# Two load slots and three store regions, and a TensorE program with a loop, in a transpose of 8192 x 8192 float32

## The chip, the cores and the metric

The kernel runs on one core of one Trainium2 chip. A core has TensorE (PE in the profile, its weight loads PEld), VectorE (DVE), ScalarE (ACT), GpSimd (POOL) and SyncE (SP), which here does nothing but issue transfers, and 16 DMA engines that move data between HBM and SBUF. The metric is the device time of one execution in microseconds (us); lower is better.

## The reference

```python
def setup_inputs():
    return {
        "x": np.random.randn(8192, 8192).astype(np.float32),
    }

def reference(x: np.ndarray) -> np.ndarray:
    return np.transpose(x)
```

256 MB are read and 256 MB written, and every element changes its place; no arithmetic is done.

## The kernel before

**Chunks and pieces.** The input is cut into T = 128 chunks. Chunk t is a block of 128 rows (block c = t % 64) by 4096 columns (half s = t // 64), 16 KB in each of 128 partitions, 2 MB; `load(t)` (L81) brings it in with one DMA. A chunk has NR = 16 pieces, one for each range r of 256 columns (J = 4096 columns, PIECE = 256 floats in a partition). TensorE transposes a piece in two matmuls against the identity (L113): one takes the even columns, one the odd, so that partition q of the result holds output rows 2q and 2q + 1, 128 columns of each. A chunk is thus 32 transposes, 16 into the PSUM tensor ps0 and 16 into ps1.

**Stores.** One piece would make output rows of just 512 bytes. So pieces of the same range r wait in the buffer `slots` (120 pieces) until 16 chunks have given theirs; `store(w)`, with r = w % 16, then writes 16 pieces as output rows of 8 KB, 2 MB in all. The ranges are staggered: with every chunk t exactly one range becomes complete, that of store t. The first 15 stores are short (1 to 15 pieces), and a flush of 15 short stores comes after the last chunk. Chunk 64 begins the second half of the columns, and the stores around it are written in two DMAs.

**What runs for chunk t.** TensorE takes the ranges in the order (t + g) % 16 for g = 0 to 15 (L112), so that the first piece, g = 0, is the one that completes store t. `gather(t)` (L196) makes VectorE copy the 15 older pieces of store t out of `slots` into a place in `arena` (L216); it first waits until the earlier store in that place has left (L203). `copies(t)` (L225) moves the new pieces out of PSUM: ScalarE those of ps0 (g = 0 to 7), VectorE those of ps1 (g = 8 to 15) (L247). Piece g = 0 goes straight into the store's place, by ScalarE; the others go to `slots`, into room that the gather has just emptied, so ScalarE first waits for the gather (semaphore s_g, L228). TensorE signals (s_pe) after 2, 4, 8, 12 and 16 pieces (`GO`), and begins each half of the next chunk when the copies have emptied that half of PSUM (L108).

**The arena.** It has NIN = 3 load slots of 16 pieces and FIN = 38 pieces for stores, a little over two full stores. A planner at build time (L152 to L167) gives every store a place in these 38 pieces, taking the one that comes free first, and lists in `before` whose end the gather must wait for. The stores of the last two chunks and of the flush may also take load slots.

**Order on SP.** SP issues every DMA, in program order on one queue, and waits in that order too (L281 to L294): store t (after the direct piece's copy, s_cl, L255), then the next load, which waits until TensorE has finished the chunk that was in its slot (L289). Up to chunk 15 and near the end this is load t + 3, whose slot chunk t has just left; between them load t + 2, whose slot chunk t - 1 left. TensorE's program is written out in full: 4096 transposes.

Of the kernel before, what the change touches and what calls it, by code (L numbers as in the profile page):

```python
# [40 lines left out]
def kernel(  # L41
# [15 lines left out]
    NIN = 3  # L57
# [3 lines left out]
    FIN = 38  # L61
    GO = (2, 4, 8, 12, 16)
    assert CH % W == 0

    with tc.tile_critical():  # L65
# [3 lines left out]
        arena = nc.alloc_sbuf_tensor("arena", [P, NIN * J + FIN * PIECE], dt).ap()  # L69
        ins = [arena[:, k * J:(k + 1) * J] for k in range(NIN)]  # L70
# [3 lines left out]
        s_ld = [nc.alloc_semaphore(f"s_ld{k}") for k in range(NIN)]  # L74
        s_st = [nc.alloc_semaphore(f"s_st{k}") for k in range(2 * W - 1)]
        s_pe = nc.alloc_semaphore("s_pe")
        s_cp = [nc.alloc_semaphore("s_cpa"), nc.alloc_semaphore("s_cpv")]
        s_g = nc.alloc_semaphore("s_g")
        s_cl = nc.alloc_semaphore("s_cl")

        def load(t):  # L81
            s, c = divmod(t, CH)
            nc.sync.dma_start(
                out=ins[t % NIN], in_=x[c * P:(c + 1) * P, s * J:(s + 1) * J]
            ).then_inc(s_ld[t % NIN], 16)

        for t in range(NIN):
            load(t)

        nc.gpsimd.memset(ident, 0.0).then_inc(s_id, 1)  # L90
        nc.gpsimd.wait_ge(s_id, 1)
        nc.gpsimd.affine_select(  # L92
            out=ident,
            in_=ident,
            compare_op=mybir.AluOpType.not_equal,
            fill=1.0,
            base=0,
            pattern=[[-1, P]],
            channel_multiplier=1,
        ).then_inc(s_id, 1)  # L100


        nc.tensor.wait_ge(s_id, 2)
        for t in range(T):
            for g in range(NR):
                h, u = divmod(g, NR // 2)
                if u == 0 and t:
                    nc.tensor.wait_ge(s_cp[h], t)  # L108
                if g == 0:
                    nc.tensor.wait_ge(s_ld[t % NIN], 16 * (t // NIN + 1))  # L110
                q = (t + g) % NR
                for b in range(B):  # L112
                    tr = nc.tensor.transpose(  # L113
                        pss[h][:, (u * B + b) * P:(u * B + b + 1) * P],
                        ins[t % NIN][:, q * PIECE + b:(q + 1) * PIECE - B + b + 1:B],
                        ident,
                    )
                if g + 1 in GO:
                    tr.then_inc(s_pe, 1)


        def lane(w):
            return w % W if w < T else W + w - T

        def parts(w):
            first, last = max(0, w - W + 1), min(w, T - 1)
            cut = [first] + [t for t in range(first + 1, last + 1) if t % CH == 0] + [last + 1]
            return list(zip(cut[:-1], cut[1:]))

        def cells(w):  # L130
            return sum(z - a for a, z in parts(w))
# [9 lines left out]

        flush = []
        for k in range((W - 1) // 2):
            flush += [T + W - 2 - k, T + k]
        flush.append(T + (W - 1) // 2)
        order = list(range(T)) + flush

        users = []
        home = {}
        before = {}  # L150
        end = NIN * NR + FIN
        for n, w in enumerate(order):  # L152
            size = cells(w)
            best = None
            low = NIN * NR if w < T - 2 else 0
            for o in range(low, end - size + 1):
                over = [(u, when) for u, a, z, when in users if a < o + size and o < z]
                for k in range(NIN):
# [133 lines left out]
        for w in flush:  # L292
            gather(w, T)
            store(w)  # L294
# [32 lines left out]
```

## Time and profile before

| | |
|---|---|
| median of 3 runs | 1276.58 us (1276.57 to 1276.77) |
| the profiled execution: its own time | 1278.0 us |
| its span, first to last instruction | 1276.2 us |
| moved by DMA | 537.53 MB, 421 GB/s over the span |
| loads | 128 of 2,048 KB, 17.2 us from issue to landing (median) |
| full stores | 98 of 2,048 KB, 13.0 us (median) |
| TensorE, VectorE, ScalarE busy | 57%, 47%, 22% of the span |
| mean granted TensorE clock | 0.741 of full speed |

Times within the profile count from the start of the span. The page gives the busy share of each engine, the span in 40 slices with the rate in GB/s, the DMA queues (q1 is SP's data queue; the queues of kind "instruction" bring the engines' code), the chain of waits that ended last, and groups of instructions by line. The trace behind it answers for stretches of the span: busy times and rate by stretch, waits by who waited for whom, instructions in order of time, and the time from issue to landing of the DMAs of one line.

### The profile page before, as it was taken

The numbers are of one execution on the slowest core, as the hardware profiler recorded it, in microseconds if no ns is written. First come the engines' busy times: TensorE is split into PE (matmuls) and PEld (weight loads), VectorE is DVE, ScalarE is ACT, GpSimd is POOL, SyncE is SP. The second block draws the span as 40 slices with busy tenths as digits, with TensorE's granted clock in tenths as the row PEclk, the third lists the DMA queues.
The fourth block names the chain that finished last, engine by engine and source line by source line (L and its number), as shares of the span: only waits on it lengthen the run. The fifth ranks groups of instructions, "written<-read, shape, count | busy, mean of one in ns | idle before, by whom it ended". The sixth has DMA issues, their size and how long they took to land.

```text
span 1276.2 us, 10252 instructions
## 1 busy us (share of the span) xinstructions
PE 731.6 (57%) x4096; PEld 711.1 (56%) x4096; DVE 600.5 (47%) x662; ACT 285.5 (22%) x513; POOL 0.7 (0%) x6
## 2 busy tenths in 40 slices
PE   5674456655665566556665665556656655555630
PEld 5664455655665556556665665556655655555630
DVE  3542644445445444454455444544454444454471
ACT  3321222222222222222222222222222222222210
POOL 0000000000000000000000000000000000000000
PEclk9987777677777777777678677686776787677765
DMA  9999999999999999999999999999999999999999
GB/s 388 428 426 388 384 429 430 430 430 430 431 430 429 427 428 429 427 420 430 415 425 421 427 427 424 422 429 430 428 426 426 425 426 423 426 425 426 424 386 375
DMA packets 41358, 537.53 MB, mean 421 GB/s; under 512 B 4576, under 2 KB 5216, under 8 KB 8288
## 3 DMA queue, kind: packets, MB, share of 16 engines
q1 hardware_dynamic: 41312, 536.89, 99.7%
q8 instruction: 32, 0.52, 0.1%
q14 instruction: 14, 0.11, 0.0%
HBM read 268.44 MB, written 268.44 MB: 421 GB/s over the span
## 4 chain that ended last, share of the span: by engine, by line
DMA 82%; PE 7%; issue 2%; DVE 2%; SPq 2%; ACT 1%; ACTq 0%; DVEq 0%
DMA arena<-in_x_dram 77%; PE ps L113 7%; DMA out_dram<-arena 5%; SPq L28 2%; ACT arena L247 1%; DVE arena L216 1%; DVE slots L247 1%; ACTq L233 0%; DVEq L212 0%; DVEq L210 0%; SPq L322 0%; DVEq L233 0%; SPq L65 0%
## 5 line engine op out<-in xcount | busy, mean ns | idle before, releaser
L113 PE MATMUL ps<-ident,arena 128*128 128x128 f32 x4096 | 731.6, 360 | 499.7 <-DMA arena<-in_x_dram 472.5
L113 PEld LDWEIGHTS ps<-ident,arena 128*128 128x128 f32 x4096 | 711.1, 218 | 519.8 <-issue 485.8
L247 DVE COPY slots<-ps 128x1024 f32<-128x1024 f32 (+3 forms) x344 | 307.6, 946 | 604.5 <-PE ps L113 604.2
L216 DVE COPY arena<-slots 128x2048 f32<-128x2048 f32 (+7 forms) x318 | 303.3, 1004 | 48.6 <-DMA out_dram<-arena 27.1
L247 ACT COPY slots<-ps 128x256 f32<-128x256 f32 (+2 forms) x384 | 249.8, 661 | 134.4 <-PE ps L113 126.7
L247 ACT COPY arena<-ps 128x256 f32<-128x256 f32 x128 | 47.6, 372 | 809.9 <-PE ps L113 722.5
L247 ACT ACT_TABLE_LOAD x1 | 1.3, 1283 | 0.9 <-SPq L65 0.9
L92 POOL TENSOR_SCALAR_AFFINE_SELECT ident<-ident 128x128 f32<-128x128 f32 x1 | 0.3, 292 | 0.2 <-POOL ident L90 0.2
L90 POOL MEMSET ident<- 128x128 f32 x1 | 0.2, 204 | 0.5 <-SPq L65 0.5
L311 POOL MEMSET const-bfloat16-1.0<- 128x1 bf16 x1 | 0.1, 101 | 0.0
L311 POOL MEMSET const-uint8-127<- 128x1 uint8 x1 | 0.1, 101 | 0.0
L311 POOL MEMSET const-float32-0.0<- 128x1 f32 x1 | 0.1, 98 | 0.2 <-issue 0.2
L311 POOL MEMSET const-float32-1.0<- 128x1 f32 x1 | 0.1, 98 | 0.0
## 6 DMA issues: line engine op xcount, KB each, us to landing
arena<-in_x_dram SPq DMA_DIRECT2D x128, 2048.0 KB, 17.2
out_dram<-arena SPq DMA_DIRECT2D x98, 2048.0 KB, 13.0
out_dram<-arena SPq DMA_DIRECT2D x4, 1920.0 KB, 11.3
out_dram<-arena SPq DMA_DIRECT2D x4, 1792.0 KB, 11.6
out_dram<-arena SPq DMA_DIRECT2D x4, 1664.0 KB, 12.7
out_dram<-arena SPq DMA_DIRECT2D x4, 1536.0 KB, 12.7
out_dram<-arena SPq DMA_DIRECT2D x4, 1408.0 KB, 13.7
out_dram<-arena SPq DMA_DIRECT2D x4, 1280.0 KB, 13.7
```

What stands on the lines that cost most here:

```text
L28: return eng.add_instruction(mybir.InstDMACopy(mode="Copy", name=nc.get_next_instruction_name(), engine=eng.engine, ins=[physical(in_)], o ...
L90: nc.gpsimd.memset(ident, 0.0).then_inc(s_id, 1)
L92: nc.gpsimd.affine_select(out=ident, in_=ident, compare_op=mybir.AluOpType.not_equal, fill=1.0, base=0, pattern=[[-1, P]], channel_multipl ...
L113: tr = nc.tensor.transpose(pss[h][:, (u * B + b) * P:(u * B + b + 1) * P], ins[t % NIN][:, q * PIECE + b:(q + 1) * PIECE - B + b + 1:B], i ...
L216: cp = nc.vector.tensor_copy(out=ap(arena, do, [[P, len(v)], [dist, B], [1, P]]), in_=ap(slots, so, [[gap, len(v)], [P, B], [1, P]]),)
L247: cp = eng.copy(out=dst, in_=i) if e == 0 else eng.tensor_copy(out=dst, in_=i)
L311: nc = _bacc.Bacc("TRN2", target_bir_lowering=False, num_devices=1)
```

## The change

1. The arena has 86 pieces as before, but another plan: two load slots of 16 pieces and 54 pieces for stores, a little over three full stores. Two more places of 16 pieces, in the store area, serve as load slots for the first chunks: up to chunk 4 loads run four ahead, up to chunk 9 three ahead, then two ahead. The store area is 22 pieces up to store 5, 38 up to store 10, and 54 from there. Stores before the flush lie in the store area; those of the flush may also take load slots.
2. SP's order: load t + 2 follows store t - 1 (before: store t). It waits until TensorE has finished chunk t, which was in its slot.
3. The planner sorts loads and stores by when they want room, and a list `before` for each names the earlier users of that room, loads and stores alike.
4. TensorE takes the ranges of a chunk in fixed order 0 to 15 (the last chunk alone is rotated as before), and signals after 4, 8, 12 and 16 pieces. So the direct piece of store t is ScalarE's when t % 16 < 8 and VectorE's otherwise, and store t waits for all of that engine's copies of chunk t (s_cpa or s_cpv). A gather waits for the copies of both engines.
5. TensorE's semaphores are counted down by TensorE itself (s_ld, and new ones, s_free, that ScalarE and VectorE raise after waiting for their own copies), so that its instructions are alike in every round. Chunks 0 to 11 are written out, a loop whose body is two chunks runs 57 times (chunks 12 to 125), and the last two chunks are written out.
6. The flush has another order: store 128 first, whose last piece also goes straight from PSUM, then 142, 129, 141, 130 and so on.

The core of the diff:

```diff
-    NIN = 3
-    FIN = 38
-    GO = (2, 4, 8, 12, 16)
+    FIN = 54
+    E = 12
+    FOUR, THREE = 5, 10
+    END = 2 * NR + FIN
+
+    def lead(t):
+        return 4 if t < FOUR else 3 if t < THREE else 2
...
+    slot_of = {ends[0][1]: 54, ends[1][1]: 70, ends[2][1]: 0, ends[3][1]: NR}
...
+    for t in range(T):
+        if t:
+            order.append(("S", t - 1))
+        while loaded <= min(T - 1, t + lead(t)):
+            order.append(("L", loaded))
+            loaded += 1
+    order += [("S", T - 1)] + [("S", w) for w in flush]
...
+    for _, k, size, until in sorted(wanted):
+        if k[0] == "L":
+            o = spot(k[1])
+        else:
+            w = k[1]
+            lo = 2 * NR if w < T - 1 else 0
+            hi = 54 if w < over[0] else 70 if w < over[1] else END
+            late = lambda o: max([f for _, a, z, f in users if a < o + size and o < z], default=0)
+            o = min(range(lo, hi - size + 1), key=lambda o: (late(o), o))
+        home[k] = o
+        before[k] = sorted({u for u, a, z, _ in users if a < o + size and o < z}, key=lambda u: due[u])
...
         def load(t):
             s, c = divmod(t, CH)
+            o = home["L", t] * PIECE
+            for u in before["L", t]:
+                free(nc.sync, u)
...
             if runs:
-                nc.vector.wait_ge(s_cp[0], upto)
-                if w >= T:
-                    nc.vector.wait_ge(s_cp[1], upto)
+                for k in range(2):
+                    nc.vector.wait_ge(s_cp[k], upto)
...
                 cp.then_inc(s_cp[e], 1)
+                if t < T - 1:
+                    eng.wait_ge(s_cp[e], t + 1)
+                    eng.sem_inc(s_free[e], 1)
 
         def store(w):
-            if w < T:
-                nc.sync.wait_ge(s_cl, w + 1)
+            if w == T - 1:
+                nc.sync.wait_ge(s_x, 1)
+            elif w < T:
+                nc.sync.wait_ge(s_cp[w % NR // (NR // 2)], w + 1)
             else:
+                if w == T:
+                    nc.sync.wait_ge(s_cp[0], T)
                 nc.sync.wait_ge(s_g, ready[w])
...
+        def transposes(t):
+            o = home["L", t]
+            for g in range(NR):
+                h, u = divmod(g, NR // 2)
+                if u == 0:
+                    nc.tensor.sem_inc(s_free[h], -1).wait_op(s_free[h], 1, "sem-ge")
+                if g == 0:
+                    nc.tensor.sem_inc(s_ld[o], -16).wait_op(s_ld[o], 16, "sem-ge")
+                q = (o + range_at(t, g)) * PIECE
...
+        nc.tensor.wait_ge(s_id, 2)
+        for t in range(E):
+            transposes(t)
...
+        with nc.body("turns", valid_engines=pe):
+            for t in range(E, E + 2):
+                transposes(t)
+            nc.regs_alu(turn, turn, 1, op=mybir.AluOpType.add)
+            nc.tensor.br_lt(turn, (T - 2 - E) // 2, on_true="turns", on_false="done")
+        nc.switch_bb("done")
+        for t in range(T - 2, T):
+            transposes(t)
```

259 lines of the change are left out of this document (144 added, 115 removed).

## The prediction

> **What bounds the kernel now.** I read the page first: the busy shares, the slices of the span and the DMA queues.
>
> ```profile
> span 1276.2 us, 10252 instructions
> PE 731.6 (57%) x4096; PEld 711.1 (56%) x4096; DVE 600.5 (47%) x662; ACT 285.5 (22%) x513; POOL 0.7 (0%) x6
> GB/s 388 428 426 388 384 429 430 430 430 430 431 430 429 427 428 429 427 420 430 415 425 421 427 427 424 422 429 430 428 426 426 425 426 423 426 425 426 424 386 375
> q1 hardware_dynamic: 41312, 536.89, 99.7%
> q8 instruction: 32, 0.52, 0.1%
> q14 instruction: 14, 0.11, 0.0%
> ```
>
> No compute engine is busy over 57% of the span, and the data queue q1 fills 99.7% of the 16 DMA engines. The 536.89 MB are input plus output, and the change moves the same bytes. So the time is bytes over rate, and a gain can only come out of slices below the best rate, which is 430 GB/s or a little over. Where they lie, I read from busy times in stretches that I cut at those slices (last column GB/s, before it the DMA share and the TensorE clock):
>
> ```profile
> core 0: us, PE busy (x) PEld busy (x) DVE busy (x) ACT busy (x) POOL busy (x), PEclk, DMA share, GB/s
> 0.00:10.00 10.00, 1.60 (x8) 1.63 (x9) 0.00 (x0) 1.74 (x3) 0.70 (x6) 1.00 0.78 315
> 10.00:100.00 90.00, 63.22 (x442) 61.08 (x440) 43.65 (x53) 27.10 (x51) 0.00 (x0) 0.91 1.01 426
> 100.00:160.00 60.00, 25.63 (x160) 25.09 (x160) 30.13 (x34) 12.52 (x24) 0.00 (x0) 0.70 0.96 383
> 160.00:400.00 240.00, 145.00 (x779) 141.16 (x780) 112.51 (x122) 54.95 (x99) 0.00 (x0) 0.73 1.01 430
> 400.00:1210.00 810.00, 481.13 (x2627) 467.88 (x2626) 384.05 (x419) 183.73 (x329) 0.00 (x0) 0.74 1.01 425
> 1210.00:1230.00 20.00, 13.73 (x81) 13.38 (x80) 10.79 (x11) 4.76 (x10) 0.00 (x0) 0.76 0.89 368
> 1230.00:1270.00 40.00, 1.30 (x7) 0.90 (x5) 19.40 (x24) 0.73 (x1) 0.00 (x0) 0.50 1.01 418
> 1270.00:1276.20 6.20, 0.00 (x0) 0.00 (x0) 0.00 (x0) 0.00 (x0) 0.00 (x0) 0.50 0.47 197
> ```
>
> Against 430 the stretches lose, length times (1 - rate/430): start 2.7 us, 10 to 100 0.8, 100 to 160 **6.6**, 160 to 400 nothing, 400 to 1210 **9.4**, 1210 to 1230 **2.9**, then 1.1 and 3.4. That is 26.9 us in all. The start (nothing to move yet), the stores alone and the last landing stay as they are, 7.2 us. The three bold ones, 18.9 us, are what this change can touch.
>
> How deep the queue is, the chain of waits shows, at its beginning and at one chunk of the good stretch, and the landings of stores there (from 160 to 400 us):
>
> ```profile
> 0.96 7.30 DMA arena<-in_x_dram
> ...
> 250.23 0.14 issue
> 250.36 1.11 PE ps L113 x4
> ...
> 251.95 0.54 SPq L28
> ...
> 252.54 17.20 DMA arena<-in_x_dram
> ```
> ```profile
> DMA to landing us min/median/max: 12.9/12.9/14.4
> ```
>
> A transfer of 2,048 KB lasts 2.097 MB / 430 = 4.88 us, so a chunk (load and store) 9.75. Into an empty queue a load landed 7.30 us after its issue. A store in the steady stretch lands after 12.9: it finds 12.9 - 7.30 = **5.6 us** of slack, queued work that runs before it is needed. Its issue comes 251.95 - 250.23 = 1.72 us after the load of its chunk landed.
>
> **The change, part by part.**
>
> *Store regions and their order (100 to 160 us).* The waits of that stretch and the row at its beginning:
>
> ```profile
> ACT arena L247 <- DVE arena L216: 49.9, 6, 15.6
> ...
> PE ps L113 <- ACT slots L247: 24.4, 2, 12.6
> DVE arena L216 <- DMA out_dram<-arena: 19.5, 2, 13.2
> ```
> ```profile
> 106.98 2.09 DVE L216 COPY arena<-slots 128x1280 f32<-128x1280 f32 x2 [13.21 <-DMA out_dram<-arena]
> ```
>
> VectorE's gather waits 13.2 us for an old store to leave its 38 pieces; ScalarE waits for the gather (its copies overwrite what the gather reads), TensorE for ScalarE, and SP's next store and load for them. The old store is late because loads sent three ahead stand before it. In the changed kernel the gather of store t reuses the place of store t-3, and load t is issued right behind store t-3. So the place is free one transfer, 4.88 us, before the data that the chunk needs anyway; the gather is two copies of 1.22 us (rows below). Exceptions are few: gathers 10 and 12 wait for a store that follows their load, of 8 and 10 pieces, 2.4 and 3.0 us by size, with two more loads queued. I leave 0.5 of the 6.6: **-6.1** (bounds 0, if a new wait takes its place, and -6.6).
>
> *Load behind the whole chunk.* With two slots load t+2 needs chunk t fully transposed, where it needed nothing that was late:
>
> ```profile
> 250.36 5.41 PE L113 MATMUL ps<-ident,arena 128*128 128x128 f32 x32 [3.07 <-DMA arena<-in_x_dram]
> ...
> 260.08 5.55 PE L113 MATMUL ps<-ident,arena 128*128 128x128 f32 x32 [4.30 <-DMA arena<-in_x_dram]
> ```
>
> It is issued 0.14 + 5.5 + 0.06 = 5.7 us after a landing, 4.0 later than the store that is now the late one, but one more transfer stands before it: slack 5.6 - 4.0 + 4.88 = 6.5 us. SP holds the next store behind this wait; that store needs the copies that follow the same transposes by 1 to 2 us, and it runs after the load. **0** in the sum; beyond 6.5 us of delay it costs each us in full. Landings should swap: loads from 17 to about 7.3 + 6.5 = 14 us, stores from 12.9 to about 16 or 17.
>
> *TensorE's loop.* The program of 4096 transposes is 4096 weight loads and 4096 matmuls; its code comes in 32 packets of 16 KB on q8. That is 256 instructions a packet, and 64 for a chunk. Looped, 12 + 2 + 2 chunks of code remain, 1024 instructions or 4 packets; 28 packets go, 0.46 MB, at 430 GB/s 1.1 us: **-1.0**. What a packet does to the engine it falls on, and the counts in both stretches, say the DMA views of 312 to 314, of 160 to 400 and of 400 to 1210 us:
>
> ```profile
> q8 instruction: 1, 0.02, 2.9%
> ```
> ```profile
> q8 instruction: 6, 0.10, 0.1%
> ```
> ```profile
> q8 instruction: 20, 0.33, 0.1%
> ```
>
> 2.9% of 16 engines in 2 us is 0.93 us on one engine. A transfer has landed when all 16 engines have done their shares, so an engine that was hit lags, the others run on, and the lags of several packets add up until the leaders run dry (beyond the 5.6 us). The spread of landings grows accordingly; the stores of 400 to 1210 us:
>
> ```profile
> DMA to landing us min/median/max: 9.6/12.9/18.7
> ```
>
> The worst is 18.7 against 14.4. From 160 to 400 us, after the first few packets, the lag costs nothing yet (430 GB/s); later it costs 9.4 us. Bounds for what removing 28 of 46 code packets returns: 0, if the 425 has another cause, to 9.4. The rest of the code packets (4 on q8, about 16 of 8 KB) are by engine time under a third of now, 2.9 us at most if the loss were linear, and the free stretch says it is not. I leave 1.5: **-7.9**.
>
> [...]
>
> *The end (1210 to 1230 us).* The last chunks' gathers wait for load slots:
>
> ```profile
> 1217.33 8.38 PE L113 MATMUL ps<-ident,arena 128*128 128x128 f32 x48 [3.49 <-DMA arena<-in_x_dram]
> ...
> 1223.83 2.35 DVE L216 COPY arena<-slots 128x1792 f32<-128x1792 f32 x2 [6.21 <-PE ps L113]
> ```
>
> In the changed kernel stores 126 and 127 have regions of their own, free since stores 123 and 124, and only the flush uses load slots. Two stores stand before the last ones when the last load lands. **-2.5** of 2.9 (bounds 0 and -2.9).
>
> *Copies, waits and the split.* A piece now goes by its range to ScalarE or VectorE, and pieces go four to a step:
>
> ```profile
> L247 DVE COPY slots<-ps 128x1024 f32<-128x1024 f32 x168 | 199.7, 1219 | 294.8 <-PE ps L113 294.6
> L216 DVE COPY arena<-slots 128x2048 f32<-128x2048 f32 x125 | 151.9, 1215 | 8.6 <-DMA out_dram<-arena 8.6
> L247 DVE COPY slots<-ps 128x512 f32<-128x512 f32 x160 | 101.6, 685 | 309.7 <-PE ps L113 309.6
> ...
> L247 DVE COPY slots<-ps 128x768 f32<-128x768 f32 x8 | 7.6, 948 | 0.0
> ...
> L247 DVE COPY slots<-ps 128x256 f32<-128x256 f32 x8 | 3.3, 415 | 0.0
> ```
>
> VectorE's copies out of PSUM become 145 of 1024, 47 of 768, 96 of 512 and 111 of 256: 176.8 + 44.6 + 65.8 + 46.1 = 333 us against 312, 0.16 us a chunk. Its busy time goes from 4.7 to 4.9 us of a chunk's 9.75: hidden. So are the added waits of each engine on its own copies (no row shows one; between nothing and the 0.4 us of a small copy, twice a chunk, of at most 1 us against 6.5 of slack). **0**; without that slack they would cost up to 1 us a chunk.
>
> **Sum.** 1276.2 - 6.1 - 7.9 - 2.5 - 1.0 = 1258.7. The profiled span is 0.4 below the median of the runs: **1259 us**.
>
> **Rivals.**
> 1. The drift stays: 425 has another cause than code packets. For it: the DMA share is 1.01 in both stretches, so the page does not show engines without work. Against: nothing else changes at 400 us. 1259 + 7.9 = 1267.
> 2. The early wait is not removed but moves: the store area is just 22 pieces up to chunk 5 and 38 up to chunk 10, no more than now. Against: two loads fewer before each store. 1259 + 6.1 = 1265.
> 3. The loop fetches its code again at every return. [...] No run here shows a branch back. The body is 2 chunks, 128 instructions. If each of 56 returns brings a packet and the wait stays under the slack, the two stalls go (-8.6), but code packets go from 46 to 76: the drift by count from 9.4 to 15.5 us (+6.1), and 28 more of 16 KB are +1.1. 1276.6 - 8.6 + 6.1 + 1.1 = 1275. Against: the body is half a packet.
> 4. **Slower.** The same returns, with the wait beyond the slack: TensorE stands at the loop's end, load t+2 cannot be issued, and the queue runs dry. It decides from 6.5 us. The longest price that a row offers is the 7.30 us of a landing: 0.8 us dry, 56 times, 45 us; with the two stalls gone, 1276.6 - 8.6 + 45 = 1313. For it: SP issues in order, so nothing else fills the queue. Against: a code packet is 0.93 us, not 2 MB.
>
> **How the numbers follow.** Forecast 0.68, rival 1 0.15, rival 2 0.05, rival 3 0.04, rival 4 0.08. About 0.2% is what a measurement of this kernel can tell from no change, 2.6 us: faster 0.88 (forecast, 1, 2), same 0.04 (3), slower 0.08 (4). The forecast's own range is 1254 (all of the bold losses back, and 431 instead of 430) to 1263 (2.9 of the drift and 2 to 3 of the stalls stay). With rivals 1 (1267) and 2 (1265), which carry the same unknowns of 1 to 3 us, the range is 1253 to 1270.
>
> **What would show it.** q8 with about 4 packets instead of 32; 428 GB/s or more from 100 to 160 and in every later slice before the end; loads landing after about 14 us and stores after 16 to 17. Rate near 425 with few q8 packets makes rival 1 true; 50 packets or more on q8, rival 3 or 4; TensorE waiting for load data with the DMA share under 0.95, rival 4. It is wrong if gathers wait over 5 us for a store in a stretch of less than 420 GB/s.

## The result, and the profile after

| | before | after |
|---|---|---|
| median of 20 runs | 1274.99 us (1272.04 to 1276.77) | 1271.44 us (1269.74 to 1276.61) |
| the profiled execution: its own time | 1278.0 us | 1270.35 us |
| its span | 1276.2 us | 1268.5 us |

The changed kernel is a little faster: ratio 0.9973, 95% interval 0.9965 to 0.9980, or 3.55 us of the medians. The forecast was 1259 us, range 1253 to 1270: the direction was right, the size was not, and the time lies above the range. Part of that is the base. The forecast started from 1276.6 us, and 20 runs put the median of before at 1275.0. The profiled executions differ by 7.7 us in their spans, more than the medians do: before's took 3.0 us longer than its median, after's 1.1 us less. The forecast for the span was 1258.7, so 9.8 us are to be found in the profile.

The page of after, in part; the last two lines are its DMA issues, with the median time from issue to landing.

```profile
span 1268.5 us, 10842 instructions
PE 739.7 (58%) x4096; PEld 719.2 (57%) x4096; DVE 615.3 (49%) x715; ACT 268.1 (21%) x402; POOL 0.7 (0%) x6
...
GB/s 394 415 426 427 431 429 430 430 430 431 432 430 430 430 431 418 432 426 422 429 423 419 427 428 430 429 420 422 425 419 423 430 423 422 430 423 425 430 421 343
...
q1 hardware_dynamic: 41312, 536.89, 100.0%
q14 instruction: 16, 0.13, 0.0%
q8 instruction: 4, 0.07, 0.0%
...
arena<-in_x_dram SPq DMA_DIRECT2D x128, 2048.0 KB, 13.8
out_dram<-arena SPq DMA_DIRECT2D x98, 2048.0 KB, 17.6
```

The hole in the fourth and fifth slices (388, 384 before) is gone. From the sixteenth slice on the rate falls below 430 again and again, as it did before, although q8 brings 4 packets of code instead of 32. The landings have swapped as forecast.

The busy times of after in the stretches that the prediction used (last column GB/s, before it the DMA share):

```profile
0.00:10.00 10.00, 1.64 (x8) 1.67 (x9) 0.00 (x0) 1.28 (x1) 0.70 (x6) 1.00 0.80 321
10.00:100.00 90.00, 64.77 (x431) 62.83 (x430) 46.81 (x57) 28.18 (x44) 0.00 (x0) 0.88 1.01 423
100.00:160.00 60.00, 37.34 (x205) 36.18 (x203) 31.98 (x38) 12.65 (x21) 0.00 (x0) 0.73 1.01 428
160.00:400.00 240.00, 144.95 (x787) 141.10 (x788) 116.75 (x134) 51.57 (x77) 0.00 (x0) 0.73 1.01 430
400.00:1210.00 810.00, 482.70 (x2629) 469.44 (x2628) 394.20 (x457) 172.28 (x257) 0.00 (x0) 0.74 1.01 426
1210.00:1230.00 20.00, 8.29 (x44) 7.93 (x42) 16.02 (x19) 2.19 (x5) 0.00 (x0) 0.67 0.99 417
1230.00:1270.00 40.00, 0.00 (x0) 0.00 (x0) 9.56 (x12) 0.00 (x0) 0.00 (x0) 0.50 0.83 344
```

As in the prediction, a stretch loses what its length exceeds the time of its bytes at 430 GB/s. A rate rounded to 1 GB/s is too coarse for this over 810 us, where half a GB/s is 0.9 us: 425 before and 426 after are in truth 425.5 both, as the bytes of the DMA views of 400 to 1210 us show (before, then after).

```profile
DMA packets 25824, 344.64 MB, mean 425 GB/s; under 512 B 2865, under 2 KB 3121, under 8 KB 4657
```
```profile
DMA packets 25837, 344.69 MB, mean 426 GB/s; under 512 B 2875, under 2 KB 3131, under 8 KB 4667
```

So the table takes the bytes that this view gives for each stretch; the last one ends with the span (46.2 us long before, 38.5 after).

| stretch | MB before | MB after | lost before, us | lost after, us | change | forecast |
|---|---|---|---|---|---|---|
| 0 to 10 | 3.15 | 3.21 | 2.7 | 2.5 | -0.1 | 0 |
| 10 to 100 | 38.32 | 38.08 | 0.9 | 1.4 | +0.6 | 0 |
| 100 to 160 | 22.95 | 25.69 | 6.6 | 0.3 | -6.4 | -6.1 |
| 160 to 400 | 103.16 | 103.30 | 0.1 | -0.2 | -0.3 | 0 |
| 400 to 1210 | 344.64 | 344.69 | 8.5 | 8.4 | **-0.1** | -7.9 |
| 1210 to 1230 | 7.36 | 8.34 | 2.9 | 0.6 | -2.3 | -2.5 |
| 1230 to the end | 17.94 | 13.77 | 4.5 | 6.5 | **+2.0** | 0 |
| code no longer fetched | | | | | -1.0 | -1.0 |

The last row is the 0.44 MB by which the bytes of the whole span fell (537.53 to 537.09). Before rounding, the changes add up to the 7.7 us of the spans. Two places explain the 9.8 us: the drift from 400 to 1210 us gave back 0.1 of a hoped 7.9, and the end took 2.0 that it had not taken before.

What happens at the end shows the DMA view of the last 20 us of each kernel, in 40 slices of 0.5 us (busy tenths of the 16 DMA engines, and GB/s). Before, then after:

```profile
DMA  9999999979999998998999999999999992000000
GB/s 383 569 379 381 416 473 518 383 301 416 416 430 475 455 401 369 471 471 334 408 422 430 420 430 453 442 387 442 387 444 412 393 442 115 16 16 0 0 0 0
```
```profile
DMA  9999989989999989999999899993311011000000
GB/s 401 408 445 436 506 373 422 453 352 401 428 418 410 504 360 471 414 406 410 426 416 461 363 487 389 393 502 139 141 78 63 33 66 49 16 16 0 0 0 0
```

Sixteen engines at 430 GB/s are 27 GB/s each. Before, all 16 work until nearly the last moment, and three slices (115, 16, 16) are left. After, the rate stays below 142 for nine slices, 4.5 us, and below 80 for seven of them: most engines have nothing left, and one to three still carry their shares. So the engines come to the end of the queue apart from each other, and the slowest sets the end. A transfer's landing is told by 16 signals: before, the first and the last of them lie 5.9 us apart at 1233 us, 2.0 at 1238 and 1.3 at the end; after, 5.1 at 1230 and 4.3 at the end. That the pause of the queue at 1210 to 1230 us had let the slow ones catch up before the change is a reading; the change also gave the last stores another order, and no run separates the two.

### The profile page after: what moved, and what is told of

It reads as the page before. It is cut to its first block, busy times and chain, and to the rows that moved or that the text cites. A ratio compares the mean times of both kernels' runs of the same rounds, so it can differ in the third digit from the quotient of the medians.

```text
span 1268.5 us, 10842 instructions
## 1 busy us (share of the span) xinstructions
PE 739.7 (58%) x4096; PEld 719.2 (57%) x4096; DVE 615.3 (49%) x715; ACT 268.1 (21%) x402; POOL 0.7 (0%) x6
## 2 busy tenths in 40 slices
DMA packets 41332, 537.09 MB, mean 423 GB/s; under 512 B 4576, under 2 KB 5216, under 8 KB 8288
## 3 DMA queue, kind: packets, MB, share of 16 engines
q1 hardware_dynamic: 41312, 536.89, 100.0%
## 5 line engine op out<-in xcount | busy, mean ns | idle before, releaser
L346 PE MATMUL ps<-ident,arena 128*128 128x128 f32 x4096 | 739.7, 363 | 482.1 <-PEq L343 482.1
L346 PEld LDWEIGHTS ps<-ident,arena 128*128 128x128 f32 x4096 | 719.2, 219 | 502.4 <-issue 502.4
L279 DVE COPY slots<-ps 128x512 f32<-128x512 f32 (+2 forms) x336 | 294.2, 915 | 537.8 <-PE ps L346 537.7
L279 ACT COPY slots<-ps 128x1024 f32<-128x1024 f32 (+2 forms) x335 | 252.7, 773 | 880.6 <-PE ps L346 832.9
L279 DVE COPY arena<-ps 128x256 f32<-128x256 f32 x63 | 26.2, 416 | 37.8 <-PE ps L346 37.8
L279 ACT COPY arena<-ps 128x256 f32<-128x256 f32 x66 | 24.8, 378 | 70.2 <-PE ps L346 55.0
## 6 DMA issues: line engine op xcount, KB each, us to landing
arena<-in_x_dram SPq DMA_DIRECT2D x128, 2048.0 KB, 13.8
out_dram<-arena SPq DMA_DIRECT2D x98, 2048.0 KB, 17.6
out_dram<-arena SPq DMA_DIRECT2D x4, 1408.0 KB, 13.8
```

What stands on the lines that cost most here:

```text
L279: cp = eng.copy(out=dst, in_=i) if e == 0 else eng.tensor_copy(out=dst, in_=i)
L346: tr = nc.tensor.transpose(pss[h][:, (u * B + b) * P:(u * B + b + 1) * P], arena[:, q + b:q + PIECE - B + b + 1:B], ident,)
```

## The experiments

The prediction blamed the code packets of TensorE's program for the drift. So the first question was what happens with the changed kernel when they come back, and whether the loop brings something of its own. Times are medians, ratios are to the kernel before, run beside it on the same chip, with the 95% interval. Kernels that were not run side by side on one chip are compared by these ratios.

**Loop undone, loop shifted.** `e1_unrolled` writes TensorE's program out in full and leaves the rest of the change; `e4_loop_cross` keeps the loop but starts it two chunks later, so that by the count of instructions its body lies across a border of two code packets (before the change 32 packets of 16 KB for 8192 instructions, 256 in each).

```diff
-        for t in range(E):
-            transposes(t)
...
-        with nc.body("turns", valid_engines=pe):
...
-        for t in range(T - 2, T):
+        for t in range(T):
             transposes(t)
```
```diff
-    E = 12
+    E = 14
```

> The changed kernel with TensorE's program written out in full, all 128 chunks without the loop; nothing else differs. Theory A (the prediction's: code packets make single DMA engines lag, and that lag is the loss after 400 us): q8 goes from 4 packets back to 32 and the time rises by 7 to 9 us over the changed kernel, to a ratio to the kernel before of about 1.003 to 1.004. Theory B (the DMA engines lag for another reason, the code packets are a small part): 0 to 2 us more than the changed kernel, a ratio of 0.997 to 0.999; the rate from 400 to 1210 us stays at 425 to 426 GB/s with 4 or with 32 packets.

> The changed kernel with 14 chunks written out before the loop instead of 12, so that by the count of instructions (64 to 67 a chunk, 256 in a code packet) the loop's body lies across a border of two code blocks. If the loop keeps the blocks on the core: q8 has 4 or 5 packets and the time is that of the changed kernel within 1 us. If a return to the earlier block fetches it again: about 56 to 112 packets on q8; by theory A 8 us or more over the changed kernel, by theory B 1 to 3 us, unless TensorE's wait at each return is over 6.5 us, which would cost 40 us and more.

Measured: `e1_unrolled` 1268.85 us, 0.9953 (0.9939 to 0.9967); `e4_loop_cross` 1270.68 us, 0.9967 (0.9955 to 0.9979). The page of `e1_unrolled` and its stretch of the drift, then the page of `e4_loop_cross` and its stretch:

```profile
q8 instruction: 33, 0.54, 0.2%
```
```profile
400.00:1210.00 810.00, 485.30 (x2644) 471.87 (x2642) 396.05 (x460) 172.83 (x258) 0.00 (x0) 0.74 1.01 428
```
```profile
q8 instruction: 4, 0.07, 0.0%
```
```profile
400.00:1210.00 810.00, 482.78 (x2629) 469.53 (x2629) 393.94 (x457) 171.83 (x257) 0.00 (x0) 0.74 1.01 425
```

Neither of the two expectations for `e1_unrolled` came true. With 33 packets of code the kernel is not slower but some 2 us faster than with 4, and by its bytes (346.89 MB) the drift loses 3.3 us, against 8.9 in `e4_loop_cross` (344.46 MB). So the code packets do not make the drift. The loop also fetches nothing again on its 56 returns: there are 4 packets in both loops. Rivals 3 and 4 fall with that.

**The transfers by themselves.** `e2_copy_shallow` leaves out the computation: 128 loads and 128 stores of 2 MB, shaped like the kernel's full ones, on the same queue, four slots of 2 MB, loads two ahead; `e3_copy_deep` has twelve slots and loads six ahead. A store writes what its load brought, untransposed.

```diff
-    LEAD, D = 2, 4
+    LEAD, D = 6, 12
```

> Only the transfers: 128 loads of 2 MB and 128 stores of 2 MB with the shapes of the kernel's full ones, from the same four slots, no TensorE, VectorE or ScalarE work, so the output is the input in blocks, not transposed. Store t waits for load t, load t+2 for store t-2; two transfers (9.75 us) stand in the queue at an issue, as in the kernel. Theory A: hardly any code packets, so no lag: 430 GB/s throughout, 2.7 us at the start, 3.4 at the end: 1250 to 1255 us. Theory B, lag without code packets: the rate falls below 430 after some hundred us as in the kernel, and the time is 1258 to 1268 us.

> As the shallow copy but twelve slots and loads six ahead, so some ten transfers (about 50 us) stand in the queue and no DMA engine can run dry for a lag of a few us. Theory A: the same time as the shallow copy. Theory B1 (the lag falls on different engines by chance, and a shallow queue turns it into idle time): 430 GB/s in the middle, 1250 to 1256 us, 6 us or more below the shallow copy. Theory B2 (always the same engine is slowest and its work sets the end): the same time as the shallow copy, with full rate in the middle and a long tail at a falling rate, where the fast engines are done.

Measured: 1256.34 us, 0.9852 (0.9837 to 0.9867), and 1256.92 us, 0.9859 (0.9844 to 0.9874). The two were run side by side. The slices on the page of `e2_copy_shallow`:

```profile
span 1255.0 us, 305 instructions
...
GB/s 379 422 425 430 429 431 430 431 431 432 430 433 430 431 432 430 432 431 431 431 430 431 430 431 431 431 432 431 430 432 431 432 431 431 432 430 431 432 431 369
```

Its stretches from 10 to 100 and from 400 to 1210 us (POOL's busy time, then the clock, the DMA share and GB/s):

```profile
10.00:100.00 90.00, 0.00 (x0) 1.00 1.01 420
...
400.00:1210.00 810.00, 0.00 (x0) 1.00 1.01 431
```

There is no drift without the computation: 430 to 433 GB/s from the sixth slice to the last but one. A longer queue adds nothing. So 1256 us is what the bytes need in full transfers, and the changed kernel is 15 us above it. (Its short stores at the start, around chunk 64 and at the end are not in the copy: 41,312 packets against 36,992 on the data queue.)

**Transfers with work beside them.** Three kernels add work to the transfers of `e2_copy_shallow`: `e5_copy_pe` the 4096 transposes (written out), `e6_copy_vec` copies on VectorE and ScalarE of about the sizes that the kernel has, `e7_copy_all` both. The work on TensorE and part of VectorE's reads each loaded chunk; a load waits for the work on the chunk four before it, which is done early enough to leave the landing of loads as it is (14.5 and 14.6 us, 14.5 in the bare transfers). The stores still write untransposed data.

> The shallow copy with TensorE's 4096 transposes added (each chunk's 32 transposes after its load; their results are overwritten in PSUM and not used; only the reuse of a load slot waits for them, which is early enough). Theory C (TensorE's work slows single DMA engines a little all the time; they lag, and the end belongs to the slowest): 1262 to 1268 us instead of 1256, with a long tail. Theory D (the work of the compute engines does not touch the transfers; what the kernel loses against the copy is lost by late issues): 1256 to 1258 us; 32 code packets at 0.9 us spread over 16 engines give at most 2.

> The shallow copy with VectorE's and ScalarE's copies added but no TensorE work: per chunk 2 copies of 2048 elements from SBUF to SBUF and 2 of 1024 from PSUM on VectorE, 2 of 1024 from PSUM on ScalarE, into an area that no DMA reads. If VectorE's and ScalarE's traffic in SBUF is what slows the DMA engines: 1260 to 1268 us; by theory C (TensorE) and theory D 1256 to 1258.

> The shallow copy with both: TensorE's transposes, then ScalarE's and VectorE's copies of their results with the waits between them, and VectorE's copies within SBUF. The same load on every engine as in the kernels, but no store waits for it. Theory C: 1263 to 1268 us, what the changed kernel without the loop takes (1268.9), so that its order and plan cost nothing more. Theory D: 1256 to 1258 us, and 11 us of the changed kernel are late issues.

Measured: 1261.39 us, 0.9899 (0.9884 to 0.9914); 1258.78 us, 0.9892 (0.9860 to 0.9924; one of six runs at 1272.09, the others up to 1259.03); 1264.44 us, 0.9920 (0.9900 to 0.9940). The slices of `e5_copy_pe`, and the last 20 us of `e7_copy_all` by slices of 0.5 us:

```profile
GB/s 379 428 427 428 430 431 431 430 431 430 430 431 430 431 430 431 431 430 430 430 430 432 431 430 430 430 430 431 429 427 431 431 428 430 431 430 431 431 426 349
...
q8 instruction: 32, 0.52, 0.2%
```
```profile
DMA  9999989999999999899999664300000000000000
GB/s 459 393 459 492 426 360 426 393 524 426 426 393 393 459 524 426 360 393 393 524 492 426 262 262 197 164 33 33 0 33 33 33 33 33 0 33 0 0 0 0
```

Against the bare 1256.34 us TensorE's work costs 5.0 us, that of VectorE and ScalarE 2.4, both 8.1, though here the stores need no result. The bare transfers were run on another chip; by the ratios (bare 0.9837 to 0.9867) the 5.0 and the 8.1 are clear, the 2.4 is not. `e5_copy_pe` has all 32 code packets and still 430 or 431 GB/s in nearly every slice, so they make no drift as deep as that of the kernel before. At the end of `e7_copy_all` a single engine brings in the last packets for some 5 us after the others (33 GB/s are one packet of 16 KB in 0.5 us). The lag of single engines that the prediction spoke of is there, then, at the end of a kernel without any loop. How much of it the code packets make and how much the work itself, these three don't tell. In the drift even `e7_copy_all`, with all the work, moves 347.74 MB, 1.3 us lost, 3.4 more than the bare transfers: the work alone does not make the 8.5 us of the kernel before.

**The changed kernel without loop and countdowns.** The loop needs semaphores that TensorE counts down and that ScalarE and VectorE raise after waiting for their own copies. `e8_lean` is `e1_unrolled` without these; TensorE waits for counts.

```diff
-                if t < T - 1:
-                    eng.wait_ge(s_cp[e], t + 1)
-                    eng.sem_inc(s_free[e], 1)
...
-                if u == 0:
-                    nc.tensor.sem_inc(s_free[h], -1).wait_op(s_free[h], 1, "sem-ge")
+                if u == 0 and t:
+                    nc.tensor.wait_ge(s_cp[h], t)
...
-                    nc.tensor.sem_inc(s_ld[o], -16).wait_op(s_ld[o], 16, "sem-ge")
+                    landed[o] += 16
+                    nc.tensor.wait_ge(s_ld[o], landed[o])
```

> The changed kernel without the loop and also without what the loop needed: TensorE waits for the counts of the copies and of the loads as before, and ScalarE and VectorE no longer wait for their own copies and raise s_free (127 waits and 127 signals on each, and 384 countdowns on TensorE, go). The plan of slots and regions and SP's order stay. If instructions as such slow the transfers: 1 to 2 us under the version without the loop, 1267 to 1268 us, a ratio of about 0.994. If the 2 us between loop and no loop come from the branch alone: the same 1268.9, ratio 0.995.

Measured: 1267.83 us, 0.9948 (0.9933 to 0.9962), the lowest of all that write the transpose.

**The early stall put back.** `e9_regions_38` is `e8_lean` with the stores 11 to 16 held to 38 pieces of the arena, as before the change.

```diff
-            hi = 54 if w < over[0] else 70 if w < over[1] else END
+            hi = 54 if w < over[0] else 70 if w < 17 else END
```

> The version without loop and countdowns (1267.8 us), but its stores 11 to 16 get 38 pieces of the store area instead of 54: the early part of the change undone. If the wait for a store region between 100 and 160 us costs what the rate loses there: the stretch falls from 429 to below 400 GB/s and the time rises by 5 to 7 us, to 1273 to 1275, so that this part is nearly all of the change's gain. If a stall there is partly handed back (the leading DMA engines wait for the lagging ones and the lag is gone): a lower rate there but only 2 to 4 us more, 1270 to 1272.

Measured: 1282.19 us, 1.0051 (1.0038 to 1.0064), more than either expectation. The stretches of `e9_regions_38` from 10 to 160 us, then those of `e8_lean`:

```profile
10.00:100.00 90.00, 64.42 (x433) 62.62 (x432) 44.76 (x55) 26.58 (x41) 0.00 (x0) 0.85 0.99 410
100.00:160.00 60.00, 26.45 (x171) 25.72 (x170) 27.51 (x34) 12.26 (x20) 0.00 (x0) 0.74 0.89 346
```
```profile
10.00:100.00 90.00, 65.98 (x439) 64.02 (x438) 46.79 (x57) 28.50 (x44) 0.00 (x0) 0.87 1.01 424
100.00:160.00 60.00, 36.71 (x200) 35.55 (x198) 31.97 (x38) 12.42 (x21) 0.00 (x0) 0.74 1.01 429
```

The first two rows lose 4.2 and 11.7 us against 430, the other two 1.4 together: the stall put back is 14.5 us. The ratios differ by 1.0051 - 0.9948 = 0.0103, or 13 us. The two kernels ran on different chips, which the section on less slack shows to be worth some us; but in the profile the later stretches of `e9_regions_38` lose no less than those of `e8_lean` (427 against 428 GB/s in the drift), so the stall is not made good later there. With loads that follow the new order the narrow arena stalls worse than before the change, 15.9 us against 7.5 from 10 to 160 us.

**The loop beside transfers that don't wait for it.** `e10_copy_pe_loop` and `e11_copy_pe_flat` transpose a constant area of SBUF beside the transfers of `e2_copy_shallow`; SP starts each round and waits for none. One has the loop of the changed kernel, the other is written out.

> The shallow copy with TensorE's 4096 transposes of a constant area, 12 chunks written out, a loop of 2 chunks 57 times, 2 chunks; SP starts each chunk's transposes when it issues the store; no transfer waits for TensorE. Against the same in full (next run). If the loop itself slows the transfers (each return costs DMA time): 2 us or more over the one written out in full. If code packets slow them (theory A's price): 1 to 3 us under it, for 28 packets less. If the 2 us of the loop arise in the kernel's chain only: the two are equal within 0.5 us.

> The same as the run before with TensorE's program written out in full: 32 code packets, no branch. Theory C: 1261 to 1263 us, as the copy with transposes of the loaded data (1261.4); with no effect of TensorE on transfers other than through the data it reads: 1256 to 1258.

Measured side by side: 1285.27 us (1274.12 to 1295.26 in 12 runs), 1.0069 (1.0047 to 1.0091), with 4 packets on q8; and 1270.61 us (1265.06 to 1277.16), 0.9968 (0.9951 to 0.9984), with 32. The kernel with the loop takes longer, though its transfers wait for nothing of TensorE, by 13 us as the ratios have it. How far that price holds elsewhere is open. Both scatter widely, and the one written out is itself 9 us above `e5_copy_pe` and above what was expected. The looped one's profiled execution was its longest run; even there the rate stays at 427 GB/s or more from the second to the twentieth slice, about 614 us, through some 25 returns:

```profile
GB/s 381 428 430 429 430 431 430 432 432 431 431 430 431 432 432 431 432 431 431 427 378 408 404 408 407 430 431 428 423 380 403 402 390 413 402 413 399 417 405 307
```

So what the loop adds is no steady price for each return.

**Less slack.** In the changed kernel load t + 2 waits for TensorE's end of chunk t. `e12_late_load` is `e8_lean` in which it waits, from chunk 20 on, for the copies of chunk t too.

```diff
+                if u[0] == "L" and t >= 20:
+                    nc.sync.wait_ge(s_cp[0], u[1] + 1)
+                    nc.sync.wait_ge(s_cp[1], u[1] + 1)
```

> The version without loop and countdowns (1267.8 us), but from chunk 20 on a load waits also for ScalarE's and VectorE's copies of the chunk that was in its slot: it is issued 1 to 2.5 us later, so loads land after about 12 us instead of 13.8 and the slack falls from 6.5 to some 4 to 5 us. If leading DMA engines that run dry set the time (the lag grows until it meets the slack, and what is beyond is lost): 3 to 6 us more, 1271 to 1274, and less than 428 GB/s from 400 to 1210 us. If only the slowest engine's own work counts: the same 1268 within 1 us, though the rate is lower in the middle and higher at the end.

Measured: 1276.88 us, 1.0016 (1.0001 to 1.0030), on the chip of the three kernels above and without `e8_lean` beside it. So it was run again on another chip beside its controls: `e13_changed_again` is the changed kernel, `e14_unrolled_again` is `e1_unrolled`, `e15_lean_again` is `e8_lean`, `e16_late_again` is `e12_late_load`.

> The changed kernel itself, beside the next three on one chip. If the loop costs time in the kernel: 1.5 to 4 us over the version written out in full (next run). If the difference of 2.6 us seen before came from the chip: equal within 0.7 us.

> The changed kernel with TensorE written out in full, beside the run before. If the loop costs time: 1.5 to 4 us less than it, with 33 code packets against 4. If code packets cost time: more than it.

> Without loop and countdowns, as control for the next run and beside the two before: 0.5 to 1.5 us under the version that is only written out in full, if the extra waits and signals cost anything; else equal.

> As the run before, but loads from chunk 20 on also wait for the copies of the chunk that was in their slot: slack 4 to 5 us instead of 6.5. If leading DMA engines that run dry cost the time: 4 to 10 us over the run before. If the end belongs to the slowest engine alone: within 1 us of it.

| | median, us | ratio (95%) |
|---|---|---|
| `e13_changed_again` | 1270.35 | 0.9957 (0.9943 to 0.9970) |
| `e14_unrolled_again` | 1268.84 | 0.9944 (0.9931 to 0.9958) |
| `e15_lean_again` | 1268.44 | 0.9943 (0.9930 to 0.9957) |
| `e16_late_again` | 1271.27 | 0.9963 (0.9949 to 0.9976) |

Their stretches from 400 to 1210 us, in that order:

```profile
400.00:1210.00 810.00, 480.79 (x2625) 467.55 (x2625) 393.82 (x457) 171.38 (x256) 0.00 (x0) 0.74 1.01 425
```
```profile
400.00:1210.00 810.00, 484.97 (x2636) 471.61 (x2635) 394.77 (x458) 172.34 (x257) 0.00 (x0) 0.74 1.01 427
```
```profile
400.00:1210.00 810.00, 487.33 (x2641) 473.90 (x2639) 395.84 (x460) 172.69 (x257) 0.00 (x0) 0.74 1.01 427
```
```profile
400.00:1210.00 810.00, 483.52 (x2615) 470.28 (x2614) 394.06 (x457) 170.45 (x254) 0.00 (x0) 0.74 1.01 424
```

The same program took 1276.88 us on one chip and 1271.27 on the other, while the kernel before took 1275.05 and 1275.58. A few us between kernels on different chips therefore prove little, which bears on `e9_regions_38`, `e10_copy_pe_loop` and `e11_copy_pe_flat` too.

The loop costs 1.5 us here (2.6 when `e1_unrolled` stands against the 20-run median), although it saves 1.0 us of code bytes. The countdown's waits cost 0.4 us, within the intervals. In `e16_late_again` the loads land after 12.2 us instead of 13.7, so the slack is 1.5 us less. That costs 2.8 us, between the two expectations: its interval overlaps that of `e15_lean_again`, but each of its five runs is longer than each of the five there. So the slack is no threshold of the kind that the prediction had.

The drift by its bytes, in all executions that bear on it, with the landing of loads and the data queue's packets of 16 KB:

| execution | TensorE's program | load landing, us | MB, 400 to 1210 us | lost, us | packets over 650 ns | their excess, us per engine |
|---|---|---|---|---|---|---|
| before | written out | 17.2 | 344.64 | 8.5 | 622 | 8.9 |
| after | loop | 13.8 | 344.69 | 8.4 | 453 | 9.0 |
| `e4_loop_cross` | loop | 13.9 | 344.46 | 8.9 | 518 | 9.7 |
| `e13_changed_again` | loop | 13.9 | 344.10 | 9.8 | 537 | 10.6 |
| `e1_unrolled` | written out | 13.7 | 346.89 | 3.3 | 209 | 4.5 |
| `e14_unrolled_again` | written out | 13.7 | 345.69 | 6.1 | 312 | 7.0 |
| `e8_lean` | written out | 13.7 | 346.98 | 3.1 | 218 | 4.1 |
| `e15_lean_again` | written out | 13.7 | 346.12 | 5.1 | 322 | 6.1 |
| `e18_lean_control` | written out | 13.7 | 346.80 | 3.5 | 205 | 4.5 |
| `e12_late_load` | written out | 12.2 | 343.82 | 10.4 | 531 | 10.6 |
| `e16_late_again` | written out | 12.2 | 343.56 | 11.0 | 542 | 10.7 |
| `e7_copy_all` | written out | 14.6 | 347.74 | 1.3 | 158 | 3.3 |
| `e5_copy_pe` | written out | 14.5 | 348.42 | -0.3 | 78 | 1.7 |
| `e2_copy_shallow` | none | 14.5 | 349.21 | -2.1 | 31 | 0.3 |

(Before the change the store is the later one, with 12.9 us. The bare transfers move a little more than 430 GB/s, hence -2.1. The excess is what the 16 KB packets took beyond 611 ns, summed and divided by 16.) The new plan without the loop loses 3.1 to 6.1 us in five executions, with the loop 8.4 to 9.8 in three, and with less slack 10.4 and 11.0. The kernel before, by its single profile, lies at the lower end of those with the loop.

The last two columns, worked out from the traces' single packets, say where the drift's time goes, and it is not where the prediction looked. The median packet of 16 KB takes 611 ns in every execution of the table, and the DMA share is 1.01 in the drift as in the bare transfers. Before the change fewer than 16 packets are in flight in just 0.8% of the drift, which makes 0.4 us for each engine; after it is the same. What grows is the time of some packets, often on several engines within a microsecond (half of the 622 before the change have at least four others that begin within 1 us of them, half of the 453 after it at least six), and their excess is about what the drift loses. So there the engines do not stand idle for want of work, as the prediction's leaders would. In the early stall of the kernel before they do, for 2.5 of its 6.6 us. What stretches the packets stays open. It may still be a form of short supply, if a packet that reaches its engine just in time lasts longer: the first 14 packets of the kernel before, which start on idle engines, took 0.71 to 1.53 us each.

**A dip at the end.** `e17_tail_dip` is `e8_lean` in which each of the stores 122 to 128 is issued only after the store two before it has landed; `e18_lean_control` is `e8_lean`.

```diff
+            if T - 6 <= w <= T:
+                nc.sync.wait_ge(s_st[lane(w - 2)], done[w - 2])
```

> The version without loop and countdowns (next run), but stores 122 to 128 are issued only when the store two before them has landed on all DMA engines. The last loads keep the lagging engine supplied with one transfer (4.9 us against some 2.4 us from issue to first data); engines that lead by 4 to 5 us run dry for 1.5 to 2.5 us. If a dip costs its share of the rate: 1.5 to 2.5 us over the next run. If only the lagging engine sets the end: within 0.7 us of it.

> The version without loop and countdowns, as control for the run before: 1267 to 1269 us.

Measured: 1268.98 us, 0.9953 (0.9939 to 0.9966), and 1268.00 us, 0.9945 (0.9932 to 0.9957). The ends of the dipped kernel and of the control:

```profile
1210.00:1230.00 20.00, 6.08 (x32) 5.92 (x32) 16.30 (x20) 2.15 (x4) 0.00 (x0) 0.63 0.93 392
1230.00:1270.00 40.00, 0.00 (x0) 0.00 (x0) 8.02 (x10) 0.00 (x0) 0.00 (x0) 0.51 0.83 343
```
```profile
1210.00:1230.00 20.00, 5.99 (x32) 5.83 (x32) 16.44 (x19) 2.15 (x4) 0.00 (x0) 0.59 1.01 429
1230.00:1270.00 40.00, 0.00 (x0) 0.00 (x0) 6.22 (x7) 0.00 (x0) 0.00 (x0) 0.53 0.74 309
```

The dip loses 20 * (1 - 392/430) = 1.8 us. After 1230 us the dipped kernel loses 5.3 us (37.2 - 40 * 343/430, its span being 1267.2) and the control 6.8 (35.5 - 40 * 309/430, span 1265.5): 1.5 are less at the end in these two executions. The medians differ by 1.0 us, which lies within the intervals and between the two expectations. That a dip shortly before the end is largely made good is what the rows suggest; the times do not settle it.

## Why the prediction was right and wrong

*What bounds the kernel.* Right. Bytes over rate, with a best rate of 430 or a little over; `e2_copy_shallow` gives 1256 us as what the bytes need in full transfers, and the losses of the table, with the code bytes, add up to the difference of the spans.

*Store regions.* Right in size, -6.4 for -6.1, and in the main in mechanism. The gathers that still wait for a store (VectorE's rows of after, with the wait in brackets) and what ScalarE waits for behind them from 100 to 160 us (total, times, longest):

```profile
71.84 1.56 DVE L243 COPY arena<-slots 128x512 f32<-128x512 f32 x2 [3.91 <-DMA out_dram<-arena]
...
87.61 1.83 DVE L243 COPY arena<-slots 128x1024 f32<-128x1024 f32 x2 [3.61 <-DMA out_dram<-arena]
...
117.12 2.35 DVE L243 COPY arena<-slots 128x1792 f32<-128x1792 f32 x2 [5.79 <-DMA out_dram<-arena]
126.55 2.36 DVE L243 COPY arena<-slots 128x2048 f32<-128x2048 f32 x2 [4.62 <-DMA out_dram<-arena]
```
```profile
DVE arena L243 <- DMA out_dram<-arena: 10.4, 2, 5.8
ACT arena L279 <- DVE arena L243: 7.4, 1, 7.4
```

The first two are gathers 10 and 12, the exceptions that the prediction named. The other two, gathers 15 and 16, it did not foresee: the planner gives stores 15 and 16 places that stores 13 and 14 had, two before and not three. They cost the rate nothing: ScalarE's wait behind them fell from 49.9 to 7.4 us, and with two loads in the queue the stretch stays at 428. `e9_regions_38` shows the other side: narrow regions stall the queue (346 GB/s from 100 to 160 us).

*Load behind the whole chunk.* The landings came out as worked out, loads 13.8 (forecast 14), stores 17.6 (16 to 17), hence a slack of 13.8 - 7.3 = 6.5 us, and no stall shows up to 400 us. The reading "free up to 6.5, then us for us" was too simple: with 1.5 us less slack the drift lost 11.0 instead of 5.1 us (`e16_late_again` against `e15_lean_again`).

*TensorE's loop: the step that failed.* The prediction read the fall from 430 to 425 after 400 us as the lag that code packets leave on single DMA engines until the leading ones run dry, and gave -7.9 for taking 28 packets away, out of a loss of 9.4 us that is 8.5 by the bytes. The packets went as counted, 28 fewer on q8, their bytes returned the -1.0, and the drift gained 0.1. Code packets do not make the drift: with 33 of them back and the new plan it loses 3.3 us (`e1_unrolled`) and 6.1 (`e14_unrolled_again`), with 4 it loses 8.4 to 9.8. A lag between engines is there: in the trace of before the time from the first to the last of the 16 landing signals of a transfer goes from 3.4 to 4.8 us with the packet of 312.5 us. But after the change it grows without packets on q8 too, from 3.8 us at 300 us to 6.0 at 480. Nor do the engines run dry in the drift (fewer than 16 packets in flight in 0.8% of it): packets take longer instead, 622 of them over 650 ns. The term also had a second error: it gave the loop no price, and by these profiles the loop takes back all that the rest of the change wins in the drift. Without it the new plan loses 3.1 to 6.1 us, with it 8.4 to 9.8, against 8.5 before the change. More slack, 6.5 us in place of 5.6, would fit that gain, and `e16_late_again` supports it with its loss for less slack; that the same slack alone would bring it in the kernel before was not tried. Why the loop costs time, and what stretches the packets, stays open. That a return of the loop fetches its code again, which rivals 3 and 4 supposed, no run shows: q8 brought 4 packets in the changed kernel and in `e4_loop_cross`.

By the prediction's own mark, a rate near 425 with few q8 packets, rival 1 came true, with a chance of 0.15 only; its 1267 us is 4 us too low. Two rows should have raised it. From 160 to 400 us six q8 packets passed without loss, which speaks as well for a lag that grows with the work as for one that grows with the packets. And the DMA share of 1.01 in the drift, which the prediction named under that rival, speaks against engines without work; in the early stall the share was 0.96.

*The end.* The stretch from 1210 to 1230 us gained 2.3 for 2.5, but the last 38 us gave 2.0 of it back. The prediction held the stores alone and the last landing fixed. They are not: every execution of the new plan loses 5.3 to 7.0 us after 1230 us, with the loop or without. Whether the missing pause or the new order of the last stores does it is open.

*Copies and waits.* VectorE's busy time grew from 600.5 to 615.3 us, hidden as forecast; the countdown's waits cost nothing that can be told (0.4 us).

*The sum.* Of the 9.8 us that the span lacks, 7.8 are the drift's term and 2.0 the end; the stretch from 10 to 100 us took 0.6 that was not forecast (423 for 426; the bare transfers have 420 there, with no work to wait for; what sets it was not tried), and others gave as much. The rest of the miss is the base, 1.6 us, and the spread of single executions.

A better version is `e8_lean`, with the new regions and order but without loop and countdowns: 1267.83, 1268.44 and 1268.00 us on three chips, 7 us under the kernel before each time. It also lies below every median of the changed kernel; side by side with it the intervals overlap.

## What to carry to other kernels

Before a drift of one per cent is given to a cause that a counter shows, run the bare transfers and add the kernel's work part by part: it tells what the floor is and which parts cannot be the cause. Take the loss of a long stretch from its bytes, not from a rounded rate: here the rounding alone turned a gain of 0.1 us into 1.9. Look whether the DMA engines stand idle before a loss is put down to engines without work. In this kernel, which fills its DMA queue, slack was worth something even while nothing waited (1.5 us less of it cost 2.8 us), and the loop in place of written-out code had to be timed, not counted by its packets (4 on q8 in place of 33, and by the medians still 1.5 us more).

## What the runs showed of the hardware

Transfers took longer beside work on the compute engines, though no store needs its result: 1256.3 us bare, 1258.8 with VectorE and ScalarE (not clear of the noise), 1261.4 with TensorE, 1264.4 with both. The difference is up to 8 us in 1256; the code packets by their time (32 of 0.93 us on one of 16 engines) would be 1.9 of the 5.0 us of TensorE, an estimate from the prediction's row of 312 to 314 us. By what way the rest comes about stays open: contention in memory, instruction fetch and semaphores were not told apart.

In the drift the 16 DMA engines nearly always had a packet in flight (fewer than 16 in 0.8% of it, before and after the change), and the DMA share was 1.01 at 425.5 GB/s as at the 431 of the bare transfers: what differed was that in the kernel before 622 packets of 16 KB took over 650 ns (the median is 611), against 31 in the bare transfers.

A kernel with a TensorE loop that fetches no code again (4 packets in 56 returns) took longer than the one written out, 1285.27 against 1270.61 us on one chip, both with wide scatter, though the transfers don't depend on TensorE. So its price is not that of code fetched again, and its cause is open too.
